# Gates among the projections, norms behind them, query norms in the exponential's scale

## The chip, the cores and the metric

The kernel runs on one core of a Trainium2 chip. The metric is the device time of one execution in microseconds, the median of the runs. The engines have the names of the profile: PE (TensorE, matrix products) with PEld (its weight loads), DVE (VectorE), ACT (ScalarE), POOL (GpSimd), and SP (SyncE), whose queue issues the DMAs here.

## What is computed

One decoder layer for 256 tokens of width 1024. Two attentions run side by side on the same normed input, eight heads each; with 256 tokens, MoBA's only block is the whole sequence, so both are plain causal attention. The gates are sigmoids of 2 x 1024 more columns of the input projection. The reference, cut:

```python
hn = rmsnorm(x, g_mix); proj = hn @ w_in       # q_a, k_a, v_a, c_q, c_kv, k_pe, gate_a, gate_b
q_a = apply_rope(rmsnorm(heads_a(q_a), moba_q_norm))
k_a = apply_rope(rmsnorm(heads_a(k_a), moba_k_norm))
y_a = moba_attention(q_a, k_a, heads_a(v_a))
q_b = rmsnorm(c_q, mla_q_lat_norm) @ w_uq       # 8 heads of 96
kv = rmsnorm(c_kv, mla_kv_lat_norm) @ w_ukv
q_b = rope_last_32(rmsnorm(q_b, mla_q_norm)); k_b = rope_last_32(rmsnorm(k_b, mla_k_norm))
y_b = causal_attention(q_b, k_b, v_b)           # softmax(q k * 96 ** -0.5) v
merged = sigmoid(gate_a) * (y_a @ w_branch_a) + sigmoid(gate_b) * (y_b @ w_branch_b)
x = x + merged @ w_out
x = x + routed_experts(rmsnorm(x, g_ffn), ...)  # top 4 of 32, softmax weights, SwiGLU of width 1024
x = x + sigmoid(rmsnorm(x, g_ple) @ w_ple_gate) * (p @ w_ple_proj)
```

## The kernel before

**Products.** Every dense product ahead of the experts is made of three (L251 to L253): both factors are split into a high part and the rest, and high by high, high by low and low by high are summed. The weights of this stage come as units of 128 x 1024 numbers or less, in the order of the table KINDS: a (the latents), q, k, u (the latents' up-projections), v, g (16 gate units), b (branches), o (output). A unit goes by DMA into a raw buffer, and make_unit splits it: ScalarE copies the high part (L210), DVE subtracts five eighths of the columns and POOL the rest for the low part (L214). The call unit(k) hands a split unit to PE and has the next ones, up to three ahead, split as far as their raw data have come; project takes four units for one projection (two token tiles, tt), gate_unit one for a tile of 128 gate columns.

**Order.** The program is written in order, and a scheduler sets each engine's queue by it and by its own estimates, so that DVE's and ScalarE's queues mix norms, splits and softmax. Before the change it runs: latents and q, the latents' norm and transposes (latT), k, MoBA's norms (moba_norm, names ha_), the up-projections uq and ukv, v, a first gate, the transposes of MoBA's q and k (moba_T, qkT), MLA's norms (mla_norm, names hb_), a second gate, and then the attention loop over j, eight pairs of heads, four of MoBA and four of MLA. One iteration emits the scores S of pair j + 1 with their softmax, a gate, the transposes PT of the probabilities of pair j (probs_T, with the copies L552 on ScalarE), a second gate, and the products O with the values (values, L562). In scores, DVE adds the mask, scales, and takes the maximum in one instruction (L534), ScalarE takes the exponentials with their sums (L538), and DVE multiplies by the reciprocal sums (L541). For j = 7 there is no gate. Then come the branch loop (br, a product for each 128 columns, with both gates), the output projection wo with the router's transposes hT, their copies on ScalarE (L630) and its logits lg (L632), and the experts.

**Memory.** Ten slots of 2 MB (ring slots) hold the stage's scratch at first. Whenever one is free, release(i) sends the next load of expert weights (w_g, w_d) into it, from the one queue of SP that also brings the units. Slot 3 is released behind the k projection, slots 6 and 5 with the attention, 4 behind it, 8 and 9 in wo. The two gate arrays, sga and sgb, and a further split tile lie in a small pool of three tiles, t8; that split tile takes the place of q and k's rows at j = 2, so that from then on (unit LAST_THREE) three split units are held, not two. The experts' own stage gives a slot back when PE has used it.

Of the kernel before, what the change touches and what calls it, by code (L numbers as in the profile page):

```python
# [65 lines left out]
def hybrid_layer(ctx, tc, x, p, b_down, w_ple_gate, w_ple_proj, bgu3, xt, tabs, wpre, wgu, wdn, out):  # L66
# [276 lines left out]
    def moba_norm(i):  # L343
        hss = wk.tile([P, 2, 8], F32, name=f"hss{i}")
        t4 = sq[:, i * 512:(i + 1) * 512]
        t3 = t4.rearrange("p (h d) -> p h d", h=8)
        for tt in range(2):
            A.square(t4, qk[:, tt, i * 512:(i + 1) * 512])
            V.tensor_reduce(hss[:, tt], t3, axis=AX.X, op=ALU.add)
        hrs = rsqrt(wk, hss.rearrange("p a b -> p (a b)"), 16, 64, "ha").rearrange("p (t h) -> p t h", t=2)  # L350
        for tt in range(2):
            src = qk[:, tt, i * 512:(i + 1) * 512].rearrange("p (h d) -> p h d", h=8)
            for u in range(2):
                G.tensor_tensor(t3[:, :, u * 32:u * 32 + 32], src[:, :, 32 - u * 32:64 - u * 32],
                                WA[i][:, tt:tt + 1, u * 32:u * 32 + 32].broadcast_to([P, 8, 32]), op=ALU.mult)
            V.tensor_tensor(src, src, CA[i][:, tt:tt + 1].broadcast_to([P, 8, 64]), op=ALU.mult)
            V.tensor_tensor(src, src, t3, op=ALU.add)
            V.tensor_tensor(src, src, hrs[:, tt].unsqueeze(2).broadcast_to([P, 8, 64]), op=ALU.mult)
# [19 lines left out]
    rbw = wk.tile([P, 2, P], F32, name="rbw")  # L378
    rbc = wk.tile([P, S], F32, name="rbc")
    for tt in range(2):  # L380
        V.tensor_scalar_mul(rbw[:, tt], ones, xrs[:, tt:tt + 1])
# [11 lines left out]
    b = bank("rbc")  # L393
    for tt in range(2):
        T.matmul(b[:, tok(tt)], rbw[:, tt], ident, start=True, stop=True)
    V.tensor_copy(rbc, b[:, :S])
# [52 lines left out]
    def mla_norm():  # L449
# [40 lines left out]


    sg = []

    def gate_unit(i):
        a, ft = divmod(i, 8)
        b = bank("gate")
        wh, wl = unit(8)
        for k in range(8):
            three([(b[:, :S], (wh[:, k], wl[:, k]), (xh[:, k], xl[:, k]))], k == 0, k == 7)
        o = sg[a].rearrange("p t (u f) -> p (t u) f", u=4)[:, ft, :]  # L500
        V.tensor_tensor(o, b[:, :S], rbc, op=ALU.mult)
        A.activation(o, o, AF.Tanh, scale=0.5)
# [96 lines left out]
    sga = sg[0].rearrange("p t (u f) -> p (t u) f", u=4)  # L599
    sgb = sg[1].rearrange("p t (u f) -> p (t u) f", u=4)  # L600
# [518 lines left out]
```

## Time and profile before

| | us |
|---|---|
| median of 3 runs | 1173.63 (1173.23 to 1173.77) |
| the profiled execution | 1168.79 |
| its span, first to last instruction | 1167.0 |
| PE, PEld busy | 1083.0, 529.2 |
| DVE, ACT, POOL busy | 337.7, 201.6, 78.5 |
| bytes moved | 440.19 MB, mean 377 GB/s |

The page splits the span into 40 slices of 29.2 us each. The attention and all dense products lie in the first seven, the experts behind them. A row of the trace names the start in us, the duration, the engine, the line of the kernel, and, in brackets, how long the engine had been idle and what it waited for; x4 is four like instructions in a row. Durations of matmuls overlap, so starts tell more of PE than durations.

### The profile page before, as it was taken

How to read it: one execution, taken by the hardware profiler on the slowest of the kernel's cores; microseconds unless marked ns; L12 is line 12 of the kernel's file. 1: busy time of each engine (PE TensorE's matmuls, PEld its weight loads, DVE VectorE, ACT ScalarE, POOL GpSimd, SP SyncE). 2: the span in 40 equal slices, each digit the busy share in tenths (PEclk: the TensorE clock that was granted, in tenths of full speed). 3: DMA queues.
4: the chain of work that ended last, by engine and by line, in shares of the span. 5: the costliest groups of instructions: out<-in, count | busy, mean ns of one | idle time of the engine just before them, and what ended most of it. 6: DMA issues, size and time to landing. Idle time of an engine off the chain costs nothing. (4 is left out here: it accounts for less than half of the span.)

```text
span 1167.0 us, 13186 instructions
## 1 busy us (share of the span) xinstructions
PE 1083.0 (93%) x5486; PEld 529.2 (45%) x5486; DVE 337.7 (29%) x754; ACT 201.6 (17%) x375; POOL 78.5 (7%) x84
## 2 busy tenths in 40 slices
PE   8879999999999999998889999998899999998988
PEld 6668997543434343342333434333333333333336
DVE  7987686321111121121110111210111111111126
ACT  6557643210000000000001000000000000000024
POOL 6553320000000000000000000000000000000000
PEclk9999999999999999999999999999999999999999
DMA  9653568799999999999999999999899999999981
GB/s 368 223 177 108 200 209 323 288 430 430 431 430 431 430 429 430 431 431 411 431 431 431 431 430 430 431 430 426 349 430 430 431 430 431 431 430 430 425 352 37
DMA packets 39650, 440.19 MB, mean 377 GB/s; under 512 B 4384, under 2 KB 5152, under 8 KB 14144
## 3 DMA queue, kind: packets, MB, share of 16 engines
q1 hardware_dynamic: 39584, 439.27, 90.2%
q8 instruction: 46, 0.75, 0.2%
q14 instruction: 20, 0.16, 0.0%
HBM read 438.21 MB, written 1.05 MB: 376 GB/s over the span
## 5 line engine op out<-in xcount | busy, mean ns | idle before, releaser
L818 PE MATMUL g<-w_g,xg 128*64 128x512 f32 x1024 | 291.3, 599 | 26.7 <-DMA w_g<-in_wgu 22.2
L818 PE MATMUL u<-w_g,xg 128*64 128x512 f32 x1024 | 288.4, 595 | 0.0
L842 PE MATMUL y<-w_d,ht 128*64 128x512 f32 x1024 | 234.5, 596 | 12.5 <-DMA w_d<-in_wdn 11.7
L822 DVE TENSOR_SCALAR g<-g 128x512 f32<-128x512 f32 x32 | 22.1, 691 | 469.0 <-PE g L812 469.0
L818 PEld LDWEIGHTS g<-w_g,xg 128*64 128x64 f32 x1024 | 77.4, 137 | 169.1 <-issue 119.8
L818 PEld LDWEIGHTS u<-w_g,xg 128*64 128x64 f32 x1024 | 81.4, 137 | 145.5 <-issue 142.2
L842 PEld LDWEIGHTS y<-w_d,ht 128*64 128x64 f32 x1024 | 72.1, 136 | 137.2 <-issue 121.2
L824 ACT ACTIVATE th<-g 128x512 f32<-128x512 f32 x32 | 20.2, 630 | 487.9 <-DVE g L822 487.9
L847 DVE COPY ys<-y 64x512 f32<-64x512 f32 x32 | 22.2, 695 | 176.0 <-ACT ys L846 176.0
L852 PE MATMUL acc<-ys,owT 128*128 128x512 f32 x128 | 59.2, 605 | 9.5 <-ACT ys L846 9.5
L846 ACT COPY ys<-y 64x512 f32<-64x512 f32 x32 | 18.5, 578 | 262.0 <-PE y L842 262.0
L852 PEld LDWEIGHTS acc<-ys,owT 128*128 128x128 f32 x128 | 23.0, 189 | 46.5 <-ACT ys L846 21.8
L779 PE MATMUL g<-oh,h_perm 128*128 128x128 f32 x256 | 33.1, 282 | 6.8 <-DVE g L822 5.6
L210 ACT CAST fr<-raw_x 128x1024 fp32r<-128x1024 f32 (+1 forms) x33 | 33.9, 1033 | 22.5 <-PE proj L253 5.9
L779 PEld LDWEIGHTS g<-oh,h_perm 128*128 128x128 f32 x256 | 29.9, 191 | 16.9 <-DVE g L822 10.6
L214 POOL TENSOR_TENSOR fr<-raw_x,fr 128x384 fp32r<-128x384 f32 (+1 forms) x25 | 34.3, 1375 | 44.8 <-ACT fr L210 37.7
L214 DVE TENSOR_TENSOR fr<-raw_x,fr 128x640 fp32r<-128x640 f32 (+2 forms) x33 | 33.0, 999 | 6.2 <-ACT fr L210 6.0
L779 PEld LDWEIGHTS u<-oh,h_perm 128*128 128x128 f32 x256 | 29.8, 192 | 8.1 <-issue 8.1
L779 PE MATMUL u<-oh,h_perm 128*128 128x128 f32 x256 | 32.2, 279 | 0.0
L252 PE MATMUL proj<-fr,fr 128*128 128x512 f32 (+1 forms) x64 | 25.8, 403 | 6.9 <-DVE fr L214 6.2
L251 PE MATMUL gate<-fr,fr 128*128 128x256 f32 x104 | 31.2, 300 | 0.0
L253 PE MATMUL gate<-fr,fr 128*128 128x256 f32 x104 | 30.1, 290 | 0.0
(317 smaller groups left out, 1133.4 us busy)
## 6 DMA issues: line engine op xcount, KB each, us to landing
w_g<-in_wgu SPq DMA_DIRECT2D x124, 2048.0 KB, 31.1
w_d<-in_wdn SPq DMA_DIRECT2D x62, 2048.0 KB, 33.5
raw_x<-in_wpre SPq DMA_DIRECT2D x38, 512.0 KB, 4.2
w_g<-in_wgu SPq DMA_DIRECT2D x8, 1024.0 KB, 28.1
raw<-in_wpre SPq DMA_DIRECT2D x8, 512.0 KB, 6.6
w_d<-in_wdn SPq DMA_DIRECT2D x4, 1024.0 KB, 19.7
w_ple<-in_w_ple_gate SPq DMA_DIRECT2D x8, 512.0 KB, 14.5
raw<-in_wpre SPq DMA_DIRECT2D x4, 416.0 KB, 7.2
```

Of the source, the lines that this page charges most:

```text
L210: A.copy(hi, src)
L214: e.tensor_tensor(lo[:, a:b], src[:, a:b], hi[:, a:b], op=ALU.subtract)
L251: T.matmul(o, lh, rh, start=first, stop=False)
L252: T.matmul(o, lh, rl, start=False, stop=False)
L253: T.matmul(o, ll, rh, start=False, stop=last)
L779: T.matmul(b[:, k * P:(k + 1) * P], h_perm[:, tt, (half * 4 + k) * P:(half * 4 + k + 1) * P], oh[:, tt], start=(tt == 0), stop=(tt == 1))
L818: T.matmul(gu[i][half * CAP:(half + 1) * CAP], xg[:, k], wv_, start=(k == 0), stop=False)
L822: V.tensor_scalar_min(g, gu[0], 7.0)
L824: A.activation(th, g, AF.Tanh, scale=0.851)
L842: T.matmul(y[g * CAP:(g + 1) * CAP], ht[:, f % 4, (f // 4) * CAP:(f // 4 + 1) * CAP], w[:, dh * 512:(dh + 1) * 512], start=(f == 0), stop= ...
L847: V.tensor_copy(ys[CAP:P, 1 - odd], y[CAP:P])
L852: T.matmul(acc[tt][dh], owT[:, dh, tok(tt)], ys[:, dh], start=first, stop=last)
```

## The change

Three things, and what follows from them:

- The 16 gate units are spread anew: one behind each of q, k and v (with latT behind v, ahead of the third), one behind the up-projections, one behind the transposes of MoBA, seven in the loop ahead of PT as before, and four (j < 4) instead of seven as second ones. For that the gates' results lie in ring slot 3, which is released behind the branch loop instead of behind k. The second further split tile is there as soon as MoBA's transposes are issued (LAST_THREE 25). In the weights' file the units lie in the new order.
- moba_norm(0) is written behind v and its gate, moba_norm(1) behind ukv; before, they stood ahead of and behind the k projection.
- The queries are not multiplied by their norm factor any more (L358 twice, L470 twice). The factor, with the softmax's scale in it, is the per-partition scale of the exponential, and the maximum is multiplied by it (scalar_tensor_tensor). The normalisation of the probabilities moves from DVE to ScalarE (A.mul).

```diff
-KINDS = (("a", 4, 832), ("q", 4, 1024), ("k", 4, 1024), ("u", 1, 1024), ("u", 1, 512), ("u", 1, 1024), ("v", 4, 1024),
-         ("g", 16, 1024), ("b", 8, 1024), ("o", 8, 1024))
+KINDS = (("a", 4, 832), ("q", 4, 1024), ("g", 1, 1024), ("k", 4, 1024), ("g", 1, 1024), ("v", 4, 1024), ("g", 1, 1024),
+         ("u", 1, 1024), ("u", 1, 512), ("u", 1, 1024), ("g", 13, 1024), ("b", 8, 1024), ("o", 8, 1024))
-N_RAW, N_EXTRA, RAW_LAST = 4, 3, 18
+N_RAW, N_EXTRA, RAW_LAST = 4, 3, 24
-LAST_THREE = 27
+LAST_THREE = 25
...
+    both_gates = slot(3, "sg")
+    sg = [both_gates[:, o:o + 2048].rearrange("p (u t) -> p u t", u=8) for o in (0, 2048)]
...
     project(512, lambda tt, b: A.mul(qk[:, tt, 0:512], b, xrs[:, tt:tt + 1]))
...
+    gate_unit()
+
+    project(512, lambda tt, b: A.mul(qk[:, tt, 512:1024], b, xrs[:, tt:tt + 1]))
...
-    moba_norm(0)
+    gate_unit()
+
+    project(512, lambda tt, b: A.mul(va[:, tt], b, xrs[:, tt:tt + 1]))
     for tt in range(2):
         b = bank("latT")
...
-    project(512, lambda tt, b: A.mul(qk[:, tt, 512:1024], b, xrs[:, tt:tt + 1]))
-    release(3)
-    moba_norm(1)
-
+    gate_unit()
...
+        if not i:
+            V.tensor_scalar_mul(hrs, hrs, 64.0 ** -0.5)
+            qscale[0] = hrs.rearrange("p (t h) -> p t h", t=2)
...
+            if i:
+                V.tensor_tensor(src, src, hrs[:, tt].unsqueeze(2).broadcast_to([P, 8, 64]), op=ALU.mult)
+
+    moba_norm(0)
...
-    project(512, lambda tt, b: A.mul(va[:, tt], b, xrs[:, tt:tt + 1]))
+    moba_norm(1)
+    gate_unit()
...
+        V.tensor_scalar_mul(brs[:, :, 0:8], brs[:, :, 0:8], 96.0 ** -0.5)
+        qscale[1] = brs[:, :, 0:8]
...
-            V.tensor_tensor(q4[:, tt], q4[:, tt], brs[:, tt, 0:8].unsqueeze(2).broadcast_to([P, 8, 96]), op=ALU.mult)
...
-        scale = (96.0 if mla else 64.0) ** -0.5
+        scale = qscale[int(mla)]
...
-                V.tensor_tensor_reduce(pr[:, c0:c1], b[:, c0:c1], mask[:, c0:c1], scale, NEG, ALU.add, ALU.max,
+                V.tensor_tensor_reduce(pr[:, c0:c1], b[:, c0:c1], mask[:, c0:c1], 1.0, NEG, ALU.add, ALU.max,
                                        mx[:, i:i + 1])
-            V.tensor_scalar_mul(mx[:, 2:4], mx[:, 0:2], -1.0)
+            h = 2 * j + u
+            V.scalar_tensor_tensor(mx[:, 2:4], in0=mx[:, 0:2], scalar=-1.0, in1=scale[:, :, h], op0=ALU.mult, op1=ALU.mult)
             for i, (c0, c1) in enumerate(sp):
-                A.activation(pr[:, c0:c1], pr[:, c0:c1], AF.Exp, bias=mx[:, 2 + i:3 + i], accum_out=mx[:, 4 + i:5 + i])
+                A.activation(pr[:, c0:c1], pr[:, c0:c1], AF.Exp, bias=mx[:, 2 + i:3 + i], scale=scale[:, i, h:h + 1],
+                             accum_out=mx[:, 4 + i:5 + i])
             V.reciprocal(mx[:, 4:6], mx[:, 4:6])
             for i, (c0, c1) in enumerate(sp):
-                V.tensor_scalar_mul(pr[:, c0:c1], pr[:, c0:c1], mx[:, 4 + i:5 + i])
+                A.mul(pr[:, c0:c1], pr[:, c0:c1], mx[:, 4 + i:5 + i])
...
-    sg.append(t8tile("sga"))
-    gi = iter(range(16))
-    gate_unit(next(gi))
     moba_T()
+    split.append(t8tile("split").bitcast(FR))
+    gate_unit()
     mla_norm()
-    gate_unit(next(gi))
     Ps = {0: scores(0, False)}
     for j in range(8):
         if j + 1 < 8:
             Ps[j + 1] = scores((j + 1) % 4, j + 1 >= 4)
         if j < 7:
-            gate_unit(next(gi))
+            gate_unit()
         pts = probs_T(Ps.pop(j))
-        if j < 7:
-            gate_unit(next(gi))
+        if j < 4:
+            gate_unit()
         values(j % 4, j >= 4, pts)
...
-            sg.append(t8tile("sgb"))
-            split.append(t8tile("split").bitcast(FR))
...
     gate_stack.close()
+    release(3)
```

What this makes of the engines' queues is seen at three places. First DVE, around the k projection; L214 are the splits, ha_ the norm of MoBA's queries and keys, hss its sums of squares, rbc the tokens' scale for the gates. Before:

```order
L214 TENSOR_TENSOR fr_81<-raw,fr_81 128x640
L97 SCALAR_TENSOR_TENSOR ha_r<-ha_t,ha_r 128x16
L356 TENSOR_TENSOR qk<-qk,pre_64 128x512
L95 TENSOR_TENSOR ha_t<-ha_r 128x16
L214 TENSOR_TENSOR fr_81<-raw_x,fr_81 128x640
L96 SCALAR_TENSOR_TENSOR ha_t<-ha_t,ha_m 128x16
L357 TENSOR_TENSOR qk<-qk,pre_64 128x512
```

and after the change:

```order
L214 TENSOR_TENSOR fr_81<-raw,fr_81 128x640
L414 TENSOR_REDUCE hss_619<-pre_64 128x8
L358 TENSOR_TENSOR sg<-gate,rbc 128x256
L88 TENSOR_SCALAR ha_m<-hss_619 128x16
L90 TENSOR_SCALAR ha_s<-ha_m 128x16
L425 TENSOR_TENSOR qk<-qk,pre_64 128x512
L214 TENSOR_TENSOR fr_81<-raw_x,fr_81 128x640
```

The norm of q still stands among the splits of the k projection's units, although it is written behind v; a gate's product is new among them.

Then ScalarE in one iteration of MLA: L552 (L572 after) are the copies of the transposed probabilities for which O waits, L565 (L585) the cast of O, L538 (L557) the exponentials of the next pair, L502 (L359) a gate's tanh. Before:

```order
L552 COPY pt<-PT 128x384 x2
L210 CAST split<-raw_x 128x1024
L502 ACTIVATE sgb<-sgb 128x256
L565 CAST fr_80<-O 128x256
L538 ACTIVATE pr,mx<-pr,mx 128x128
L538 ACTIVATE pr,mx<-pr,mx 128x256
L538 ACTIVATE pr,mx<-pr,mx 128x128
L538 ACTIVATE pr,mx<-pr,mx 128x256
L210 CAST fr_81<-raw_x 128x1024
L502 ACTIVATE sgb<-sgb 128x256
L552 COPY pt<-PT 128x384 x2
```

and after:

```order
L210 CAST split<-raw_x 128x1024
L585 CAST fr_80<-O 128x256
L557 ACTIVATE pr,mx<-pr,mx,hb_r 128x128
L557 ACTIVATE pr,mx<-pr,mx,hb_r 128x256
L557 ACTIVATE pr,mx<-pr,mx,hb_r 128x128
L561 ACTIVATE pr<-pr,mx 128x128
L561 ACTIVATE pr<-pr,mx 128x256
L557 ACTIVATE pr,mx<-pr,mx,hb_r 128x256
L359 ACTIVATE sg<-sg 128x256
L561 ACTIVATE pr<-pr,mx 128x128
L561 ACTIVATE pr<-pr,mx 128x256
L572 COPY pt<-PT 128x384 x2
```

The four normalisations L561 now stand between the exponentials of the next pair and the copies of the present one, and one split and one tanh of the second gate are gone.

Last ScalarE in the output projection: fss are sums of squares, L630 (L646) the router's copies of hT. Before:

```order
L210 CAST fr_80<-raw_x 128x1024
L653 ACTIVATE sq,fss<-xs 128x512 x2
L210 CAST fr_80<-raw_x 128x1024
L630 COPY raw_x<-hT 128x4x128 x2
L653 ACTIVATE sq,fss<-xs 128x512 x2
```

and after:

```order
L669 ACTIVATE sq,fss<-xs 128x512
L210 CAST fr_80<-raw_x 128x1024
L646 COPY raw_x<-hT 128x4x128 x2
L210 CAST fr_80<-raw_x 128x1024
L669 ACTIVATE sq,fss<-xs 128x512 x2
```

The last unit's split has moved behind the first two copies. On SP's queue the load of slot 3, which stood among the loads of the v units, now stands between the fourth and the fifth unit of wo.

## Rows read from the trace of the kernel before

**Rows 1.** The page: bytes in 40 slices, and a group of DMA issues.
```profile
GB/s 368 223 177 108 200 209 323 288 430 430 431 430 431 430 429 430 431 431 411 431 431 431 431 430 430 431 430 426 349 430 430 431 430 431 431 430 430 425 352 37
...
w_g<-in_wgu SPq DMA_DIRECT2D x124, 2048.0 KB, 31.1
```

**Rows 2.** Waits of PE from 222 us: total, times, longest, in us.
```profile
PE g L818 <- DMA w_g<-in_wgu: 22.2, 21, 2.4
```

**Rows 3.** Timeline of SP's queue: start, duration, line, transfer.
```profile
185.80 0.33 SPq L80 DMA_DIRECT2D raw_x<-in_wpre  x1
...
221.99 0.33 SPq L80 DMA_DIRECT2D w_g<-in_wgu  x1
```

**Rows 4.** Windows: length, busy PE, PEld, DVE, ACT, POOL, PEclk, DMA share, GB/s.
```profile
43.36:46.76 3.40, 3.40 (x10) 2.49 (x9) 2.83 (x5) 0.62 (x1) 2.39 (x3) 0.50 0.50 157
...
196.96:200.36 3.40, 3.40 (x14) 3.01 (x14) 0.08 (x1) 0.58 (x1) 0.00 (x0) 0.50 0.99 417
65.00:69.00 4.00, 3.93 (x17) 3.19 (x18) 4.00 (x6) 1.87 (x3) 2.87 (x2) 1.00 0.75 217
...
202.00:222.00 20.00, 18.15 (x132) 13.86 (x132) 10.52 (x49) 6.72 (x9) 0.00 (x0) 1.00 0.57 229
```

**Rows 5.** Timeline of PE in the projections of k and v.
```profile
42.67 0.50 PE L252 MATMUL proj<-fr,fr 128*128 128x512 f32 x1 [2.17 <-DVE fr L214]
...
57.68 0.50 PE L252 MATMUL proj<-fr,fr 128*128 128x512 f32 x1 [0.97 <-DVE fr L214]
...
65.07 0.50 PE L252 MATMUL proj<-fr,fr 128*128 128x512 f32 x1 [1.65 <-DVE fr L214]
```

**Rows 6.** Timeline from MoBA's transposes to the first read of scores (L534).
```profile
73.33 1.91 PE L436 MATMUL qkT<-cst,qk 128*128 128x128 f32 x16
...
78.11 1.85 DVE L214 TENSOR_TENSOR fr<-raw_x,fr 128x640 fp32r<-128x640 f32 x1
...
82.04 0.81 DVE L214 TENSOR_TENSOR fr<-raw_x,fr 128x640 fp32r<-128x640 f32 x1
...
83.66 0.28 DVE L534 CUSTOM_DVE_ANT_0 pr<-S,mask 128x128 f32<-128x128 f32 x1
```

**Rows 7.** Timeline of one iteration of MLA, O to O.
```profile
131.55 0.66 PE L562 MATMUL O<-pt,scr 128*64 128x256 f32 x4
...
134.71 0.40 ACT L538 ACTIVATE pr<-pr,mx 128x128 f32<-128x128 f32 x1 [1.50 <-DVE mx L536]
...
136.39 0.18 ACT L538 ACTIVATION_READ_ACCUMULATOR pr<-pr,mx 128x1 f32 x1
...
137.22 0.36 PE L251 MATMUL gate<-fr,fr 128*128 128x256 f32 x1
...
140.26 0.66 PE L562 MATMUL O<-pt,scr 128*64 128x256 f32 x4
```

**Rows 8.** Timeline of the last pair: copies, and O.
```profile
151.16 0.86 ACT L552 COPY pt<-PT 128x384 f32<-128x384 f32 x2
...
151.69 0.81 PE L562 MATMUL O<-pt,scr 128*64 128x256 f32 x3 [1.10 <-ACT pt L552]
```

**Rows 9.** Timeline of the router's products in the output projection.
```profile
196.33 1.38 PE L632 MATMUL lg<-cst,raw_x 128*128 128x32 f32 x8 [1.55 <-ACT raw_x L630]
```

**Rows 10.** Lines, 20 to 155 us: busy, mean ns; idle before.
```profile
L452 DVE TENSOR_REDUCE bss<-pre 128x8 f32<-128x768 f32 x2 | 1.9, 936 | 0.0
...
L468 DVE TENSOR_TENSOR qb<-qb,pre 128x768 f32<-128x768 f32 x2 | 2.7, 1348 | 0.1
...
L541 DVE TENSOR_SCALAR pr<-pr,mx 128x256 f32<-128x256 f32 x16 | 5.5, 347 | 0.0
...
L398 ACT ACTIVATE qk<-proj,x_r 128x512 f32<-128x512 f32 x2 | 1.4, 678 | 4.0 <-PE proj L253 4.0
...
L411 ACT COPY qb<-uq 128x512 f32<-128x512 f32 x2 | 1.1, 580 | 0.0
```

**Rows 11.** Timeline of the first gate product of MLA with the late split tile.
```profile
115.98 0.19 PEld L251 LDWEIGHTS gate<-fr,split 128*128 128x128 f32 x1 [1.10 <-ACT split L210]
```

More of the change, by code (lines that the diff above doesn't have):

```diff
@@ L340, in hybrid_layer, with gate_unit @@
         WB.append(w)
[L343 to L358, printed above, removed]
-    project(512, lambda tt, b: A.mul(qk[:, tt, 0:512], b, xrs[:, tt:tt + 1]))
+    both_gates = slot(3, "sg")
+    sg = [both_gates[:, o:o + 2048].rearrange("p (u t) -> p u t", u=8) for o in (0, 2048)]
+    gi = iter(range(16))
+    def gate_unit():
+        a, ft = divmod(next(gi), 8)
+        b = bank("gate")
+        wh, wl = unit(8)
+        for k in range(8):
+            three([(b[:, :S], (wh[:, k], wl[:, k]), (xh[:, k], xl[:, k]))], k == 0, k == 7)
+        o = sg[a][:, ft, :]
+        V.tensor_tensor(o, b[:, :S], rbc, op=ALU.mult)
+        A.activation(o, o, AF.Tanh, scale=0.5)
+    project(512, lambda tt, b: A.mul(qk[:, tt, 0:512], b, xrs[:, tt:tt + 1]))
+    rbw = wk.tile([P, 2, P], F32, name="rbw")
+    rbc = wk.tile([P, S], F32, name="rbc")
+    for tt in range(2):
+        V.tensor_scalar_mul(rbw[:, tt], ones, xrs[:, tt:tt + 1])
+    b = bank("rbc")
+    for tt in range(2):
+        T.matmul(b[:, tok(tt)], rbw[:, tt], ident, start=True, stop=True)
+    V.tensor_copy(rbc, b[:, :S])
+    gate_unit()
+    project(512, lambda tt, b: A.mul(qk[:, tt, 512:1024], b, xrs[:, tt:tt + 1]))
     G.tensor_tensor(w_r, w_r, gkp.unsqueeze(2).broadcast_to([P, 8, NE]), op=ALU.mult)
@@ L375, in hybrid_layer @@
         V.tensor_scalar_mul(lsq[:, tt, 256:384], lr[:, tt, 256:384], lrs[:, 2 * tt + 1:2 * tt + 2])
[L378 to L381, printed above, removed]
-    moba_norm(0)
+    gate_unit()
+    project(512, lambda tt, b: A.mul(va[:, tt], b, xrs[:, tt:tt + 1]))
     for tt in range(2):
@@ L392, in hybrid_layer, with moba_norm @@
         V.tensor_tensor(latl[:, :, tok(tt)], lf, lath[:, :, tok(tt)], op=ALU.subtract)
[L393 to L396, printed above, removed]
-    project(512, lambda tt, b: A.mul(qk[:, tt, 512:1024], b, xrs[:, tt:tt + 1]))
-    release(3)
-    moba_norm(1)
+    gate_unit()
+    qscale = [None, None]
+    def moba_norm(i):
+        hss = wk.tile([P, 2, 8], F32, name=f"hss{i}")
+        t4 = sq[:, i * 512:(i + 1) * 512]
+        t3 = t4.rearrange("p (h d) -> p h d", h=8)
+        for tt in range(2):
+            A.square(t4, qk[:, tt, i * 512:(i + 1) * 512])
+            V.tensor_reduce(hss[:, tt], t3, axis=AX.X, op=ALU.add)
+        hrs = rsqrt(wk, hss.rearrange("p a b -> p (a b)"), 16, 64, f"ha{i}")
+        if not i:
+            V.tensor_scalar_mul(hrs, hrs, 64.0 ** -0.5)
+            qscale[0] = hrs.rearrange("p (t h) -> p t h", t=2)
+        hrs = hrs.rearrange("p (t h) -> p t h", t=2)
+        for tt in range(2):
+            src = qk[:, tt, i * 512:(i + 1) * 512].rearrange("p (h d) -> p h d", h=8)
+            for u in range(2):
+                G.tensor_tensor(t3[:, :, u * 32:u * 32 + 32], src[:, :, 32 - u * 32:64 - u * 32],
+                                WA[i][:, tt:tt + 1, u * 32:u * 32 + 32].broadcast_to([P, 8, 32]), op=ALU.mult)
+            V.tensor_tensor(src, src, CA[i][:, tt:tt + 1].broadcast_to([P, 8, 64]), op=ALU.mult)
+            V.tensor_tensor(src, src, t3, op=ALU.add)
+            if i:
+                V.tensor_tensor(src, src, hrs[:, tt].unsqueeze(2).broadcast_to([P, 8, 64]), op=ALU.mult)
+    moba_norm(0)
     qb = t8tile("qb")
@@ L489, in mla_T @@
                 A.copy(qbT[0:96, 2 * hh:2 * hh + 2, :], b[0:96].rearrange("p (h t) -> p h t", h=2))
[L492 to L502, printed above, removed]
     att_stack = ExitStack()
@@ L596, in hybrid_layer @@
     release(4)
[L599 to L600 removed]
+    sga, sgb = sg
     mT = [xh, xl]
@@ L1088, in _layout @@
     tiles = lambda a: [a[:, :, n:n + P].reshape(P, -1) for n in range(0, 1024, P)]
[L1089 to L1091 removed]
+    gates = tiles(w[:, :, 1952:2976]) + tiles(w[:, :, 2976:4000])
+    pieces = [cols(1536, 1952), cols(0, 512), gates[0], cols(512, 1024), gates[1], cols(1024, 1536), gates[2],
+              uq[:, :, 0:512].reshape(P, -1), uq[:, :, 512:768].reshape(P, -1), i["w_ukv"][0]]
+    pieces += gates[3:] + tiles(br.reshape(P, 8, D))
     pieces += [wo[:, :, 512 * n:512 * n + 512].reshape(P, -1) for n in range(2)]
```

3 lines of the change are left out of this document (removed).

## The prediction, made before the change was timed

> **What bounds the kernel now.** I read the page's slices first: the row of bytes stands at about 430 GB/s from the ninth slice (233 us) nearly to the end, and before it at 108 to 368 [rows 1]: memory is the limit of the second part, and not of the first. Of PE's waits behind 222 us the largest is the expert matmuls' for a load, 22.2 us in 21 times [rows 2]. The DMA issues show what starts this stream: loads between units of the output weights, as the one of 185.80, and then the expert load of 221.99, the first that follows a matmul of an expert [rows 3]. Between 202 and 222 the DMA engines were 57% busy, so 8.6 us idle [rows 4]. From 222 on the bytes that are left decide, and they are the same in both kernels. So the time is the moment at which the first expert gives back a slot, plus a constant: a microsecond won on PE's path before 222 is a microsecond of the kernel, and nothing behind it can be won by this change.
>
> PE's path ahead of 222 has these holes. In the k projection the matmul at 42.67 waits 2.17 us for DVE's part of a split, L214, and from 43.36 the granted clock is 0.50 for 3.40 us [rows 4, 5], which costs 1.7 us more (1.2 GHz in place of 2.4). In the v projection the waits are 0.97 and 1.65 us, and the clock stays, 1.00 behind the longer [rows 4, 5]. The first scores are read by DVE at 83.66 [rows 6], and PE waits for them. Later, up to 148.91, PE is nearly full, two gate products to each pair of heads, and one iteration of MLA takes 8.71 us (O at 131.55, next O at 140.26) [rows 7]. Two holes follow: 1.10 us at 151.69 for the copies of the last pair, and 1.55 us at 196.33, where the router's products wait for ScalarE, with half clock from 196.96 for 3.40 us [rows 4, 8, 9].
>
> **The change, part by part.** All terms are microseconds of PE's path; plus is a gain. One gate product takes 3.04 us (137.22 to 140.26) [rows 7]. There are 16 in both kernels.
>
> *Gates among the projections, norms later.* Before, 4 gates are done when the third pair's scores end; after, 7: 9.1 us of work done earlier. Against it stands how much later the first scores are read. The transposes qkT started at 73.33 [rows 6]. Three more gates ahead of them add 9.1. The k projection's hole goes if its splits are made while PE does a gate (2.17 + 1.7 = 3.9), and so do the two in v (0.97 + 1.65 = 2.6) [rows 5]. The latents' transposes now stand behind v, close ahead of their reader, and no row of before shows that wait: it lies between 0 and the six DVE operations of 384 columns in that step, 3.1 by the 0.347 of 256 columns [rows 10]; I take 1.9, above the middle, since DVE is hardly free in that stretch. That puts qkT at 73.3 + 9.1 - 3.9 - 2.6 + 1.9 = 77.8. From qkT to the first read of scores were 10.33 us [rows 6], spent on MLA's sums of squares on DVE, with two splits among them, 1.85 and 0.81. After, no split stands in that stretch of DVE's order, but one sum L452 and one product L468 more than before, 0.936 and 1.348 [rows 10]: 10.33 - 2.66 = 7.7 if these two find idle time, 9.95 if not, 10.3 if nothing is won. I take 9.4, nearer to the upper ones, since they stand in the chain: 77.8 + 9.4 = 87.2, which is 3.5 later than 83.66. **Gain 9.1 - 3.5 = 5.6**; bounds 1.7 (k's hole stays) and 9.2 (no wait for the latents, and 7.7). MoBA's two query products L358 lie in the stretch of k and v, where they belong to what made the splits late, and MLA's two L470 behind the first read; I don't count them again. From the first read to the first O I let things stay as they were, since the new normalisation on ScalarE only takes the place of DVE's there.
>
> *Second split tile from the start.* At 115.98 PE's weight load waits 1.10 us, since that tile is made only inside the loop and its first split is late [rows 11]. **Gain 1.0.** ScalarE has the same casts as before.
>
> *MLA's iterations with one gate.* For j = 4, 5 and 6 PE has 8.71 - 3.04 = 5.67 us of work, and now the ring through the other engines decides: ScalarE takes its instructions in order, and the four normalisations L561 of the next pair stand ahead of the copies for which PE waits. O to the first exponential 3.16 (131.55 to 134.71; S, the cast of O, a split and the read of the scores lie in it); four exponentials 1.86 (134.71 to the last reading of a sum, 136.39, and its 0.18); four normalisations at the same, without the readings, of which half shows: 1.86 - 4 x 0.09 = 1.5; first copy to O 0.53 (151.16 to 151.69) [rows 7, 8]. Sum 7.05. The reciprocal on DVE between a head's exponentials and its normalisations costs the first head nothing, since an exponential of the second stands between; for the second it lies between 0, if the gate's tanh covers it, and a hand-over as from copy to O, 0.53. The exponentials get a second operand per partition: L398 with one takes 0.678 and L411 without 0.580 for 512 columns [rows 10], so 0 to 4 x 0.1. I take the one in full and the other at 0, or both at about half: 7.6, between 7.05 and 7.98. That is 1.93 longer than PE's work, three times: **loss 5.8**; bounds 4.1 and 6.9, and 0 if the normalisations hide. In MoBA's iterations a ring of that length stays below PE's work with two gates, so there it costs nothing; without that cover it would cost the same. What DVE is spared, 0.347 for 256 columns [rows 10], it had time for there.
>
> The Trainium skill speaks against this edit: "ScalarE: Activation LUTs", section "Rules for kernel authors", sends plain multiplications to VectorE, not to ScalarE; the row of L541 and the 1.5 for four agree with it. The same page, section "What ACT_TABLE_LOAD costs", adds about 93 ns for each operand per partition, as the two rows do; by it alone the ring would be 7.95, the loss 6.8 and the time 1171.6.
>
> *The end of attention.* In the last iteration no tanh of a gate stands ahead of the copies any more, and the 1.10 at 151.69 shrinks to a few tenths [rows 8]: **gain 0.7**, between 0 and 1.1.
>
> *The wo stage.* ScalarE's router copies now stand ahead of the last unit's split, not behind it; before, that split waited for the load issued at 185.80, and the hole cost 1.55 + 1.7 = 3.2 [rows 3, 4, 9]. But slot 3, which now holds the gates, gets its expert load here, between wo's units on the one queue of SP: 2048 KB at 430 GB/s [rows 1] are 4.9 us in front of the last units. Bounds -0.5 (the units come so late that PE waits 3.7 for them) and +3.2 (they come in time); I take the middle, **gain 1.5**. The bytes themselves fit in the 8.6 us that are idle there.
>
> Sum: 5.6 + 1.0 - 5.8 + 0.7 + 1.5 = **3.0**. The profiled execution took 1168.79, which is 4.84 below the median of 1173.63; its like after would take 1165.8, and the median **1170.6**.
>
> **The rivals.** (1) *Slower: ScalarE's line, and the clock with it.* Of the waits of 2.17 and 1.55 each was followed by half clock, that of 1.65 was not; the 1.9 of each MLA iteration lies among these. At half clock a gate ends 1.7 later, and its tanh, which stands ahead of the second head's normalisations, with it: 7.6 becomes 9.3. With a split that is slow on DVE (1.85 for the form of 0.81, [rows 6]) it is over 10. From 9.4 on it decides: at 9.5, 3 x 3.83 = 11.5 are lost, and the whole is 3.0 + 5.8 - 11.5 = 2.7 slower, 1176.3. For it speak these waits; against it that PE would still be full for most of each iteration. (2) *Wash: the splits stay late.* If the norms' operations stand ahead of the splits on DVE all the same, and the order after shows some of them there, the k projection keeps its hole: 1.7 in place of 5.6, sum -0.9, 1174.5. That is also the case in which the change doesn't do what it says. (3) *More gain.* If with an emptier DVE the read of scores comes 1.0 sooner in the 3.16, the ring is 6.6, the loss 2.8 and the sum 6.0: 1167.6. For it: DVE has less to do; against it: the cast of O and the split still stand ahead of the read.
>
> **How the numbers follow.** Forecast 40%, (1) 18%, (2) 20%, (3) 22%. A measurement of this kernel can tell 0.2%, 2.35 us: faster is below 1171.3, slower above 1176.0. The forecast's own range is 1168.5 to 1172.6, two thirds of it faster; (3) is faster, nine tenths of (2) and a seventh of (1) are within. Together 0.48 faster, 0.34 the same, 0.18 slower. The range for 8 in 10 goes from (3) with somewhat more of the early gain, 1166.0, to (1), 1176.5.
>
> **What would show it.** Right: a k projection of about 11 us without a row of half clock; the first read of scores near 87; MLA's O to O at 7.6 with waits for ScalarE's copies of 1.9, three times; the load of the first returned slot near 219. Wrong: an O to O of 9 and more, or below 7; a fall of the clock in MLA's iterations; the k hole still there; wo's matmuls waiting for a load of a unit.

## The result, and the profile after

The changed kernel takes 1179.96 us (median of 5 runs, 1177.12 to 1181.76), before 1173.63; the ratio is 1.0054, 95% interval 1.0040 to 1.0069. It is 6.3 us slower. The prediction was 1170.6 with a range of 1166.0 to 1176.5: the sign is wrong, and the time lies outside the range. The profiled execution of after is the fastest of its five, 1177.12 with a span of 1175.1; against the profiled one of before that is 8.1 us of span. The profiled one of before lies 4.84 below its median and that of after 2.84, so 2 of these 8 us are how the two executions fell, and the traces below explain 8 and not 6.3.

The first view is the page of after, its slices of bytes and its busy time of PE. As in [rows 1], the bytes stand at 430 GB/s from the ninth slice on.

```profile
PE 1086.0 (92%) x5486; PEld 529.3 (45%) x5486; DVE 330.2 (28%) x720; ACT 215.9 (18%) x407; POOL 76.1 (6%) x84
...
GB/s 371 212 150 101 163 184 289 318 432 430 429 431 430 430 431 429 431 430 410 432 429 431 430 431 430 431 431 427 346 431 431 429 432 429 430 433 429 427 356 36
```

SP's queue in after, as [rows 3]: the last unit of wo, and the load into the first slot that an expert gives back.

```profile
194.21 0.33 SPq L80 DMA_DIRECT2D raw_x<-in_wpre  x1
...
230.04 0.33 SPq L80 DMA_DIRECT2D w_g<-in_wgu  x1
```

That last load comes at 230.04, not at 221.99: 8.05 us later, and the span is 8.1 us longer. So all of the loss lies ahead of the experts. Read off the starts of PE's (and DVE's) rows in both traces:

| moment | before | after | later by |
|---|---|---|---|
| first read of scores | 83.66 | 90.68 | 7.0 |
| first O (4 gates done before, 7 after) | 92.94 | 101.66 | 8.7 |
| fourth O (j = 3) | 122.91 | 130.88 | 8.0 |
| seventh O (all 16 gates done) | 148.91 | 155.07 | 6.2 |
| branch products start | 152.87 | 158.59 | 5.7 |
| wo starts | 176.54 | 184.17 | 7.6 |
| last matmul of wo starts | 204.58 | 212.63 | 8.0 |

With a gate at 3.04 us, the terms of the prediction against this table:

| term | predicted | measured | from |
|---|---|---|---|
| three gates earlier, scores later | +5.6 | +0.4 | 9.1 - 8.7 |
| split tile (first to fourth O) | +1.0 | +0.8 | 30.0 to 29.2 |
| three iterations of MLA | -5.8 | -7.3 | 26.0 - 9.1 = 16.9 to 24.2 |
| end of attention (O to br) | +0.7 | +0.4 | 3.96 to 3.52 |
| branch products | 0 | -1.9 | 23.7 to 25.6 |
| wo | +1.5 | -0.4 | 28.0 to 28.5 |
| sum | +3.0 | -8.0 | |

Each trace is one execution. The run with the loads in wo held back (below) has the kernel of before up to wo; its trace has the first O at 93.72, the branch products at 154.76 and wo at 179.37, which is 0.8, 1.9 and 2.8 later than in the trace of before. So a single term of about 1 us is within what two executions of the same work differ by. The 5.2 by which the early term fell short, and the 7.3 of MLA, are well above that.

The timeline of after up to the first transposes answers [rows 5, 6]:

```profile
45.99 0.50 PE L252 MATMUL proj<-fr,fr 128*128 128x512 f32 x1 [1.37 <-DVE fr L214]
...
62.34 0.50 PE L252 MATMUL proj<-fr,fr 128*128 128x512 f32 x1 [1.88 <-DVE fr L214]
...
80.01 0.27 PE L466 MATMUL qkT<-cst,qk 128*128 128x128 f32 x1
...
90.68 0.28 DVE L552 CUSTOM_DVE_ANT_0 pr<-S,mask 128x128 f32<-128x128 f32 x1
...
93.89 0.33 PE L570 MATMUL PT<-cst,pr 128*128 128x128 f32 x1 [4.52 <-ACT pr L561]
...
96.23 0.48 PE L570 MATMUL PT<-cst,pr 128*128 128x128 f32 x1 [1.25 <-ACT pr L561]
```

The hole of k is smaller, 1.37, and its half clock is gone. That of v is not: it is 1.88 where the two of before were 0.97 and 1.65, and now half clock follows. The transposes for the second head wait once more, 1.25, for ScalarE's normalisation. The windows (columns as in [rows 4]; the third is all that lies ahead of the first read) show the clock, and DVE's work:

```profile
63.41:66.81 3.40, 3.40 (x11) 2.61 (x10) 3.26 (x9) 1.52 (x3) 1.16 (x1) 0.50 0.57 165
94.13:100.95 6.82, 5.50 (x25) 5.01 (x25) 4.37 (x15) 5.93 (x20) 0.00 (x0) 0.50 0.45 126
...
0.00:90.68 90.68, 80.26 (x444) 67.43 (x444) 74.01 (x138) 52.08 (x79) 55.52 (x69) 0.98 0.66 241
```

The same window of before, up to its own first read:

```profile
0.00:83.66 83.66, 72.27 (x372) 58.62 (x372) 69.85 (x133) 46.33 (x72) 48.90 (x64) 0.98 0.71 261
```

DVE has 4.2 us more to do ahead of the first read (74.01 for 69.85), although query products were taken from it: three gates bring three splits and three products of 256 columns with them. The order of DVE's work has changed too. Before, MLA's sums of squares began 5.6 us ahead of qkT (73.33 [rows 6]):

```profile
67.69 0.94 DVE L452 TENSOR_REDUCE bss<-pre 128x8 f32<-128x768 f32 x1
```

After, the up-projections stand behind v, and the sums begin with qkT (80.01). They are behind splits in DVE's queue, for which DVE sits idle until ScalarE has cast them:

```profile
74.72 0.83 DVE L214 TENSOR_TENSOR fr<-raw,fr 128x640 fp32r<-128x640 f32 x1 [2.57 <-ACT fr L210]
...
79.10 0.82 DVE L214 TENSOR_TENSOR fr<-raw,fr 128x640 fp32r<-128x640 f32 x1 [1.99 <-ACT fr L210]
79.85 0.95 DVE L482 TENSOR_REDUCE bss<-pre 128x8 f32<-128x768 f32 x1
...
81.65 1.39 DVE L214 TENSOR_TENSOR fr<-raw_x,fr 128x640 fp32r<-128x640 f32 x1
```

From qkT to the first read DVE then has no gap: it is busy for 10.64 of 10.67 us, before for 7.83 of 10.33.

MLA's iterations in after, to be read beside [rows 7]: four O's, and the copies that the second waits for.

```profile
130.88 0.44 PE L582 MATMUL O<-pt,scr 128*64 128x256 f32 x2
...
139.15 0.46 ACT L572 COPY pt<-PT 128x384 f32<-128x384 f32 x1
...
139.66 0.43 PE L582 MATMUL O<-pt,scr 128*64 128x256 f32 x1 [2.86 <-ACT pt L572]
...
147.36 0.43 PE L582 MATMUL O<-pt,scr 128*64 128x256 f32 x1 [1.49 <-ACT pt L572]
...
155.07 0.43 PE L582 MATMUL O<-pt,scr 128*64 128x256 f32 x1 [1.42 <-ACT pt L572]
```

O to O is 8.78, 7.70 and 7.71, against 5.67 of PE's work; the wait names ScalarE's copies each time. In the branch products and in wo, PE now waits here:

```profile
178.28 0.39 PE L253 MATMUL br<-fr,fr 128*128 128x256 f32 x1 [1.35 <-DVE fr L214]
...
200.72 0.51 PE L251 MATMUL wo<-fr,fr 128*128 128x512 f32 x1 [1.61 <-ACT fr L210]
```

### The profile page after: what moved, and what is told of

Its sections match the earlier page's. It is cut to its first block, busy times and chain, and to the rows that moved or that the text cites. A ratio compares the mean times of both kernels' runs of the same rounds, so it can differ in the third digit from the quotient of the medians.

```text
span 1175.1 us, 13158 instructions
## 1 busy us (share of the span) xinstructions
PE 1086.0 (92%) x5486; PEld 529.3 (45%) x5486; DVE 330.2 (28%) x720; ACT 215.9 (18%) x407; POOL 76.1 (6%) x84
## 3 DMA queue, kind: packets, MB, share of 16 engines
HBM read 438.21 MB, written 1.05 MB: 374 GB/s over the span
## 5 line engine op out<-in xcount | busy, mean ns | idle before, releaser
L795 PEld LDWEIGHTS g<-oh,h_perm 128*128 128x128 f32 x256 | 29.9, 191 | 16.9 <-DVE g L838 10.6
L214 DVE TENSOR_TENSOR fr<-raw_x,fr 128x640 fp32r<-128x640 f32 (+2 forms) x29 | 30.1, 1040 | 14.1 <-ACT fr L210 14.0
L210 ACT CAST fr<-raw_x 128x1024 fp32r<-128x1024 f32 (+1 forms) x29 | 29.9, 1035 | 19.4 <-PE proj L253 9.1
L251 PE MATMUL gate<-fr,fr 128*128 128x256 f32 x104 | 31.6, 304 | 0.0
L253 PE MATMUL gate<-fr,fr 128*128 128x256 f32 x104 | 30.4, 292 | 0.8 <-DVE fr L214 0.7
L252 PE MATMUL proj<-fr,fr 128*128 128x512 f32 (+1 forms) x64 | 25.6, 401 | 5.4 <-DVE fr L214 4.9
L252 PE MATMUL gate<-fr,fr 128*128 128x256 f32 x104 | 30.2, 290 | 0.0
```

The costliest lines, as they stand in the source:

```text
L210: A.copy(hi, src)
L214: e.tensor_tensor(lo[:, a:b], src[:, a:b], hi[:, a:b], op=ALU.subtract)
L251: T.matmul(o, lh, rh, start=first, stop=False)
L252: T.matmul(o, lh, rl, start=False, stop=False)
L253: T.matmul(o, ll, rh, start=False, stop=last)
L795: T.matmul(b[:, k * P:(k + 1) * P], h_perm[:, tt, (half * 4 + k) * P:(half * 4 + k + 1) * P], oh[:, tt], start=(tt == 0), stop=(tt == 1))
```

## The experiments

All ratios are to the kernel before, on the same chip, with 95% intervals. Theory A: in iterations with one gate, ScalarE's in-order line decides; and in wo, the expert loads that stand ahead of the last units. Theory B: DVE's queue ahead of the first scores decides, and the gates lengthen it. Theory C, for wo: ScalarE's order, not the loads.

### The normalisations back on DVE, and the fold undone

```diff
-                A.mul(pr[:, c0:c1], pr[:, c0:c1], mx[:, 4 + i:5 + i])
+                V.tensor_scalar_mul(pr[:, c0:c1], pr[:, c0:c1], mx[:, 4 + i:5 + i])
```

> The changed kernel with one part undone: the four normalisations of a pair's probabilities are DVE's again. Theory A (ScalarE's in-order line is what costs time): without them MLA's O to O falls from 8.78, 7.70 and 7.71 us to 6.0 to 6.4, the waits of O for the copies go from 6.4 us in all to under 2, the first transposes wait 1 to 2 us less, and the time is 1171 to 1174. Theory B (the scores come late whoever normalises, because norms, splits and gates share DVE): O to O stays above 7.2 and the time is 1178 or more.

Measured: 1174.15, ratio 1.0027 (1.0006 to 1.0047). O to O in MLA:

```profile
137.98 0.43 PE L582 MATMUL O<-pt,scr 128*64 128x256 f32 x1 [0.30 <-ACT pt L572]
...
145.48 0.43 PE L582 MATMUL O<-pt,scr 128*64 128x256 f32 x1 [0.68 <-ACT pt L572]
...
152.06 0.43 PE L582 MATMUL O<-pt,scr 128*64 128x256 f32 x1 [0.30 <-ACT pt L572]
```

The first of these follows an O at 131.77, so 6.21, 7.50 and 6.58: 20.3 for three and not 24.2. The waits of O are under 1 us. About half of the loss goes (1.0054 to 1.0027, with intervals that overlap a little). Two of the iterations are longer than A's 6.4, and the time does not go below before: the first read is at 93.36, 2.7 later than in after, although DVE, ScalarE, POOL and PE have the same instructions in the same order up to qkT in both. A wait in v, of 1.90 here and 1.88 in after, was followed by half clock in after and not here. PE then comes to the latents' products earlier and waits for DVE there, 0.94 and once more 0.92, which the trace of after does not have:

```profile
70.01 0.47 PE L251 MATMUL uq<-fr,fr 128*128 128x512 f32 x1 [0.94 <-DVE fr L401]
```

Half clock follows these waits in their turn (71.69 to 75.10).

With the fold undone and the normalisations left on ScalarE:

```diff
...
+            V.tensor_tensor(q4[:, tt], q4[:, tt], brs[:, tt, 0:8].unsqueeze(2).broadcast_to([P, 8, 96]), op=ALU.mult)
...
-        scale = qscale[int(mla)]
+        scale = (96.0 if mla else 64.0) ** -0.5
...
```

> The changed kernel with the other part undone: queries are multiplied by their norm on DVE again, the exponential has one per-partition operand; the normalisations stay on ScalarE. Theory A: each exponential is 0.1 us shorter, four in a ring, so MLA's O to O is 7.3, 1.2 us less in three iterations; DVE has 3.3 us more to do, part of it ahead of the first read of scores: in all 1178 to 1182, as the changed kernel. If the exponential's second operand were the main cost: 1176 or less.

Measured: 1178.23, ratio 1.0049 (1.0034 to 1.0063), as A expected: within the interval of the changed kernel. MLA's O to O are 7.28, 7.58 and 7.65, the first and the second ending here:

```profile
137.52 0.65 PE L575 MATMUL O<-pt,scr 128*64 128x256 f32 x2 [1.36 <-ACT pt L565]
...
145.10 0.43 PE L575 MATMUL O<-pt,scr 128*64 128x256 f32 x1 [1.36 <-ACT pt L565]
```

With both undone, so that only the gates' places (and the order of norms, slot 3 and the split tile) are changed:

> The changed kernel with fold and normalisations both undone, so the gates' places alone. Theory A+B: MLA's O to O is 6.0 to 6.4, as no normalisation stands ahead of the copies, but the first read of scores stays at 91 to 94 and wo has its longer wait: the ratio to before is 1.001 to 1.004, the same as with the normalisations alone undone (1.0027). If the gates' places are good by themselves: below 0.999.

Measured: 1173.24, ratio 1.0014 (0.9994 to 1.0034). The ratio is as expected; the iterations are not. They take 7.00, 7.30 and 7.37:

```profile
137.75 0.43 PE L575 MATMUL O<-pt,scr 128*64 128x256 f32 x1 [1.08 <-ACT pt L565]
...
145.05 0.43 PE L575 MATMUL O<-pt,scr 128*64 128x256 f32 x1 [1.09 <-ACT pt L565]
```

So even without a normalisation on ScalarE the ring is longer than PE's work: in this order a split's cast (1.05) and the gate's tanh (0.41) stand between the exponentials and the copies. The three iterations take 21.7, with the normalisations alone undone 20.3, in the changed kernel 24.2, and PE's work in them is 16.9. The four normalisations lengthen a ring that holds PE up already.

### Fold and normalisation without the gates' places

The kernel before with the normalisations on ScalarE alone; with the fold alone; with both:

> The kernel before with one part of the change alone: normalisations on ScalarE, all gates where they were, two in each iteration. Theory A: PE's 8.7 us of work in an iteration cover the ring of 7.3 us, so only the first transposes and the last pair lose 1 to 2 us: 1174 to 1176. If the normalisations stand in the way even there: O to O over 9, 1180 or more.

> The kernel before with the query norms folded into the exponential's scale, and nothing else of the change. DVE has four products less, 3.3 us, and each exponential is 0.1 us longer. Theory B (DVE sets the time to the first scores): the first read comes 0.5 to 1.5 us sooner than 83.66, the iterations stay at PE's 8.7 us, the time is 0.5 to 2 us lower than before: 0.9983 to 0.9996 of it. If the fold costs by itself: above 1.001.

> The kernel before with the fold and the normalisations on ScalarE, so the whole change but the gates' places (and what goes with them: slot 3, the split tile, the order of norms and projections). Theory A+B (the gates' places are what costs: thin iterations of MLA expose ScalarE's line, and the projections fill DVE ahead of the first scores): O to O stays at 8.7 us, the first read at 83 to 84, and the ratio to before is 0.999 to 1.003. If fold and normalisation cost by themselves when together: 1.004 or more.

Measured: 1173.03, ratio 1.0003 (0.9986 to 1.0020); 1173.36, 1.0011 (0.9999 to 1.0024); 1173.43, 1.0018 (1.0003 to 1.0033). With the normalisations on ScalarE and two gates an iteration, O to O stays at 8.64, 8.71 and 8.65, without a wait:

```profile
132.03 0.65 PE L562 MATMUL O<-pt,scr 128*64 128x256 f32 x3
...
140.74 0.44 PE L562 MATMUL O<-pt,scr 128*64 128x256 f32 x2
```

That is theory A's cover. The fold did not bring the first read forward as B expected: 83.50 for 83.66. Taken together, the gates' places alone are +0.14%, the rest alone +0.18%, and the whole +0.54%. The 0.2% left over, 2.5 us, would be there only with both; but each of the three intervals is 0.15 to 0.2% to either side, so the times alone do not show that it is more than nothing. That the normalisations cost with one gate an iteration and not with two is read from the iterations.

### Where the gates stand

The four second gates in the iterations j = 3 to 6, so that MLA has two and MoBA one:

```diff
-        if j < 4:
+        if 3 <= j < 7:
             gate_unit()
```

> The changed kernel with the four second gates in the iterations j = 3 to 6 and not 0 to 3, so MLA's have two each and MoBA's first three one. Theory A (any iteration with one gate is held by ScalarE's line of 7.0 to 7.7 us, whichever attention it is): the first three O to O grow from nothing lost to 7.0 to 7.6 against PE's 5.3, MLA's are 8.7 without a wait, and the time is within 2 us of the changed kernel's, ratio 1.004 to 1.008. If only MLA's longer scores make the ring: MoBA's are below 6.2 and the ratio is below 1.002.

Measured: 1179.64, ratio 1.0070 (1.0045 to 1.0095). The O's of j = 1, 2 and 4:

```profile
108.93 0.65 PE L582 MATMUL O<-pt,scr 128*64 128x256 f32 x2 [1.36 <-ACT pt L572]
...
116.65 0.43 PE L582 MATMUL O<-pt,scr 128*64 128x256 f32 x1 [1.89 <-ACT pt L572]
...
139.41 0.44 PE L582 MATMUL O<-pt,scr 128*64 128x256 f32 x2
```

The waits have moved with the gates: MoBA's O to O are 9.11 (partly at half clock) and 7.72, MLA's first two 8.64 and 8.71. So any iteration with one gate is held by the ring, as A says, whichever attention it is.

One gate from behind the up-projections to iteration j = 4:

```diff
     moba_norm(1)
-    gate_unit()
...
-        if j < 4:
+        if j < 5:
             gate_unit()
```

> The changed kernel with one gate product moved from behind the up-projections to the second place of iteration j = 4, the first of MLA with one gate. Theory A: the iteration from the third O to the next has room for it, 1 us longer at most, while MoBA's transposes start 2.9 us sooner and the first read of scores comes 2 to 3 us sooner: 1177 to 1178.5. Theory B: DVE is the limit ahead of the first read, which comes as late as now, and the gate is 1 us of loss: 1181.

Measured: 1185.07, ratio 1.0108 (1.0073 to 1.0144): worse than either theory had it. The first read came at 89.32, 1.4 us sooner than in after, though qkT started 2.7 us sooner (77.3). DVE is not full in between: it is idle for 3.94 us, waiting for ScalarE's cast of a split that stands in its queue ahead of MLA's sums.

```profile
81.23 0.83 DVE L214 TENSOR_TENSOR fr<-raw,fr 128x640 fp32r<-128x640 f32 x1 [3.94 <-ACT fr L210]
```

So DVE's queue sets the first read here too, but by a wait in it and not, as B has it, by its load. PE then ran out of work:

```profile
94.20 0.47 PE L569 MATMUL PT<-cst,pr 128*128 128x128 f32 x1 [7.52 <-ACT pr L560]
...
98.40 0.47 PE L569 MATMUL PT<-cst,pr 128*128 128x128 f32 x1 [3.11 <-ACT pr L560]
```

and the window behind it is at half clock for 13.64 us, with PE busy half of the time:

```profile
90.63:104.27 13.64, 6.95 (x30) 6.12 (x30) 9.37 (x40) 8.41 (x27) 0.51 (x1) 0.50 0.36 116
```

### DVE ahead of the first read

The changed kernel without the rotation of MLA's queries on DVE:

```diff
-            V.tensor_tensor(q4[:, tt], q4[:, tt], CB[0][:, tt:tt + 1].broadcast_to([P, 8, 96]), op=ALU.mult)
-            V.tensor_tensor(q4[:, tt, :, 64:96], q4[:, tt, :, 64:96], rt2, op=ALU.add)
```

> The changed kernel without the rotation of MLA's queries on DVE (its product with the cosines and the sum, four operations, 2.9 us of DVE between the transposes qkT and the first read of scores); the result is not the layer's. Theory B (DVE's queue sets when the scores are read): the first read comes 2.5 to 2.9 us sooner than 90.68, at about 88, and PE's wait for the first transposes shrinks by as much; time 1176 to 1177.5. If PE's transposes or ScalarE set it, the first read stays at 90 to 91 and the time at 1179 or more.

Measured: 1180.08, ratio 1.0060 (1.0040 to 1.0079). The first read moved as B says and somewhat more, to 87.09, though qkT started at 80.6; PE's wait for the first transposes fell from 4.52 to 2.22:

```profile
87.09 0.28 DVE L550 CUSTOM_DVE_ANT_0 pr<-S,mask 128x128 f32<-128x128 f32 x1
...
92.17 0.33 PE L568 MATMUL PT<-cst,pr 128*128 128x128 f32 x1 [2.22 <-ACT pr L559]
...
148.35 0.43 PE L580 MATMUL O<-pt,scr 128*64 128x256 f32 x1 [1.36 <-ACT pt L570]
```

The time did not follow: the O of 148.35 comes 10.73 us after that of 137.62, and the window between is at half clock:

```profile
138.75:145.56 6.81, 6.81 (x29) 6.41 (x28) 2.85 (x13) 3.44 (x12) 1.64 (x1) 0.50 0.57 207
```

So theory B is right on the first read, where DVE had no gap behind qkT. Its time was wrong: in the profiled execution the gain of 2.4 us at the first O (99.30 for 101.66) was more than lost again in one iteration of MLA, which took 3.0 longer than in after.

### The loads in wo

The changed kernel with slot 3's load behind wo's units:

```diff
-    release(3)
+    seen = wk.tile([P, 1], F32, name="seen")
...
+        if dh == 0:
+            G.tensor_tensor(seen, both_gates[:, 0:1], xs[:, 0, 0:1], op=ALU.add)
+            release(3)
```

> The changed kernel with the load of slot 3 held back: one small POOL operation that reads the gates and the first half of wo's result stands ahead of it, so the 2048 KB go behind all units of wo. Theory A (that load delays wo's units, and PE waits 1.76 and 1.03 us in wo for it): wo's wait for ScalarE's split falls to the 1.5 of the kernel before or below, and the time is 1 to 3 us lower, 1177 to 1179. Theory C (the stall is only ScalarE's order): the wait stays at 1.8 or more and the time is as the changed kernel's, 1180.

Measured: 1180.33, ratio 1.0084 (1.0051 to 1.0117), against theory A. One expert load still stands ahead of the last unit, and ScalarE's order went back to that of before, with the copies for the router behind the last split:

```profile
195.49 0.38 SPq L80 DMA_DIRECT2D w_g<-in_wgu  x1
197.60 0.33 SPq L80 DMA_DIRECT2D raw_x<-in_wpre  x1
...
208.79 0.30 PE L648 MATMUL lg<-cst,raw_x 128*128 128x32 f32 x1 [2.22 <-ACT raw_x L646]
```

The wait moved from wo's matmul to the router's, 2.22 us, and wo takes 28.0 for 28.5. This run alone doesn't tell A from C. So next all loads were held back, first in the kernel before:

```diff
-    def release(*slots):
+    def release(*slots, dep=None):
...
+            if dep is not None:
+                G.tensor_copy(t[:, 0:1], dep)
...
-            for after, i in ((1, 8), (3, 9)):
-                if 4 * dh + kk == after:
-                    release(i)
+            if 4 * dh + kk == 2:
+                release(8, dep=split[0].bitcast(F32)[:, 1, 0:1])
+                release(9, dep=split[0].bitcast(F32)[:, 1, 1:2])
```

> The kernel before with one thing of its own mended: the loads into slots 8 and 9 wait (by one number that POOL writes into them) until unit n = 47 is split, so the last unit of wo is loaded ahead of them. If PE's path ahead of the experts passes into the time one to one, the 1.55 us of waiting and the 1.7 us of half clock at 196 go, and the time is 2.5 to 3.2 us lower than before, 0.9973 to 0.9979 of it. If the expert loads that now start 3 us later are what counts: not lower than before.

Measured: 1166.82 (1165.66 to 1169.22), ratio **0.9951** (0.9933 to 0.9968): faster than both kernels. The two loads now follow the last unit, and the router's wait is 0.66 for 1.55 [rows 9]:

```profile
189.28 0.80 SPq L80 DMA_DIRECT2D w_g<-in_wgu  x2
...
198.22 0.30 PE L634 MATMUL lg<-cst,raw_x 128*128 128x32 f32 x1 [0.66 <-ACT raw_x L632]
...
222.30 0.33 SPq L80 DMA_DIRECT2D w_g<-in_wgu  x1
```

wo takes 25.5 us, not 28.0, and no half clock follows it. The gain in the time, 5.7 us (3.8 to 7.9), is above the 2.5 to 3.2 that was expected. The profile does not explain the rest: it is of the slowest of the four runs (1169.22), with half clock in the attention, where the kernel is unchanged. Its slot load, at 222.30, comes no sooner than the 221.99 of before, whose trace is of an execution 4.84 below the median. That part stays open.

The same in the changed kernel, with slot 3's load too:

> The changed kernel with the loads into slots 3, 8 and 9 held back until unit n = 47 is split, so that all units of wo are loaded ahead of them, as in the run on the kernel before. Theory A (PE waits in wo for the last units, which come late behind expert loads): the waits of 1.61 and 0.76 us in wo go, wo takes 25.5 to 26.5 us and not 28.5, and the ratio to before falls from 1.0054 to 1.001 to 1.0035; still slower than before, since attention's loss stays. If the stall there is a matter of ScalarE's order: wo stays above 27.5 us and the ratio at 1.005.

Measured: 1176.51, ratio 1.0036 (1.0020 to 1.0053). wo takes 25.8 us, not 28.5, and the longest wait in it is this:

```profile
PE wo L254 <- DVE fr L216: 0.6, 1, 0.6
```

So A holds for wo: it is the expert loads ahead of the last units. The trace of after says the same of its wait of 1.61 at 200.72: the cast that PE waits for stood on ScalarE for the unit's load, and not behind other work.

```profile
199.62 1.04 ACT L210 CAST fr<-raw_x 128x1024 fp32r<-128x1024 f32 x1 [3.10 <-DMA raw_x<-in_wpre]
```

## Why the prediction was wrong

**What bounds it: right.** In all fourteen profiles the load into the first slot that comes back stands at 221.99 to 238.47, and the span less that moment is 944.8 to 947.2 (945.0 before and after). A microsecond of PE ahead of the experts is one of the kernel, within those 2.4.

**The early term, +5.6 and measured +0.4, was the step that failed.** It moved DVE's work as a chain that hangs on qkT, and took the holes in k and v for something that three gates on PE would fill. Of the 5.2 us that are missing, 2.2 lie ahead of qkT (80.0 and not 77.8), 1.3 between qkT and the first read (10.67 and not 9.4), and 1.7 behind it (10.98 to the first O and not 9.28).

Ahead of qkT, k's hole shrank by 2.5 in place of 3.9, and that of v, which was to go, grew by 1.0: 1.88 and 1.7 for the half clock behind it, for 2.62. A gate is no pure work of PE. Each brings a split of 0.8 to 1.6 and a product of 0.4 to DVE, which was busy for 27.2 of the 30 us from 37 to 67, and DVE's work up to the first read rose by 4.2. The 1.9 for the latents was well judged, but does not stand beside the half clock: with the normalisations on DVE these waits are 0.94 and 0.92, and in after, where PE comes later after half clock, they are not there. All nine profiles with the gates moved show one or the other: half clock behind v's wait of 1.9 (six), or the two waits for the latents (three).

Behind qkT the prediction had no split left in DVE's order, and counted one sum and one product more, in part hidden in idle time. A split of 1.39 stands there (81.65), so do both sums and both products, and there is no idle time. The idle time lies ahead of qkT, where DVE waits for ScalarE's casts; in all it rose by 2.9 (16.7 for 13.8). The run with less DVE work moved the first read by 3.6 us.

Behind the first read the prediction left things unchanged; its list of holes leaves out that PE waited 4.43 for the first transposes before (87.35), with half clock from 87.72 to 91.13. In after that wait is 4.52. The second head's transposes wait 1.25 more for ScalarE, and half clock lasts 6.82 us and not 3.4. The clock may be most of this: in the run on the kernel before with wo's loads held back, where the attention is unchanged, half clock lasts 6.82 too, and that stretch takes 10.42.

**MLA, -5.8 and measured -7.3: the ring was right, its size a little too small, its cause half right.** 7.6 was forecast for O to O; two of three are 7.70, and the first, 8.78, has two casts of splits ahead of O's cast. What was wrong is the bound "0 if the normalisations hide": with them on DVE the three iterations still take 20.3 to 21.7 us for 16.9 of PE's work, so of the 7.3 between 3.4 and 4.8 is there without them. The second operand per partition made each exponential 0.09 longer (L538 before, L557 after). The Trainium skill ("ScalarE: Activation LUTs", "What ACT_TABLE_LOAD costs") gives about 93 ns for each such operand; the trace agrees.

```profile
L538 ACT ACTIVATE pr<-pr,mx 128x256 f32<-128x256 f32 x16 | 7.9, 495 | 0.0
...
L538 ACT ACTIVATE pr<-pr,mx 128x128 f32<-128x128 f32 x16 | 6.3, 397 | 10.5 <-DVE mx L536 10.4
```

```profile
L557 ACT ACTIVATE pr<-pr,mx,hb_r 128x256 f32<-128x256 f32 x8 | 4.7, 586 | 0.0
L557 ACT ACTIVATE pr<-pr,mx,hb_r 128x128 f32<-128x128 f32 x8 | 3.9, 489 | 6.0 <-DVE mx L555 6.0
```

**wo, +1.5 and measured -0.4.** The forecast took the middle between bounds; the lower one, late units, was nearly what happened (-0.5). Slot 3's load stands behind the fifth unit of wo (189.13), and with that of slot 8 (192.16) two loads stand ahead of the last unit, before one. **The branch products, 0 and measured -1.9,** were not thought of; PE waits 1.35 for a split on DVE at 178.28. In the fourteen profiles that stretch takes 23.1 to 26.4 us with the same work; what sets it was not settled.

**The rivals.** Rival (1), ScalarE's line with the clock, is nearest in its time, 1176.3, at 18%, but by luck. In the profiled execution its clock part did not happen in MLA (no half clock from 101 us to the end of wo); the ring made 7.3 of loss without it, and the early gain that was to pay for a ring of 7.6 did not come. In three profiles of changed variants half clock did fall in MLA, with iterations of 9.21 (slot 3 late), 10.73 (less DVE) and 10.75 (gate moved). That such falls also make the 2.8 us between the profiled execution and the median of after is likely, and not shown. Rival (2), the wash with the splits late, had the early term at +1.7; it too was too high.

## What to carry to other kernels

A piece of work that is moved on one engine carries its helpers on the others with it: count what the moved unit puts on every engine ahead of the point it is to speed up, add that to the load of the one that has no gaps, and look for what in that engine's queue now waits for another engine ahead of the work that matters.

When the products that fill PE's time are thinned out, a ring through the other engines can come to light. Add it up beforehand, instruction by instruction, in the order of the slowest in-order queue, and see whether it is below the work that is left even without the rest of the change.

A queue that serves small urgent loads and large early ones in order is worth a look by itself: here, holding two early loads back by a few microseconds gained 0.5%, and the change as a whole lost as much.

## What was not expected of the hardware

Half clock did not follow from the length of the single wait ahead of it: a wait of 1.88 was followed by it (after, 62.34), and one of 1.90 at the same matmul was not (normalisations on DVE, 62.61); one of 2.03 was (less DVE, O at 137.62), one of 2.86 was not (after, 139.66). Ahead of the experts it came in stretches of 3.40, 6.82, 10.24 and 13.64 us. And one kernel's executions differ by up to 9 us (1169.44 to 1178.84 in ten of the run with normalisations on DVE), so that a third of a per cent needs its interval.
